# A decoder layer whose first projection (v) gets leading transposes, a paired tile order, VectorE sums and a separate pool for two convolution tiles

## The chip, the cores and the metric

The kernel runs on one core of a Trainium2 chip. The metric is device time in microseconds (us) of one execution; lower is better. TensorE multiplies matrices into the eight banks of PSUM, VectorE and ScalarE do element-wise work, GpSimd does element-wise work on SBUF only, and SyncE (SP) issues every DMA of this kernel, in order, in one queue. Within each engine instructions run in a fixed order.

## The reference, cut to what matters

One layer: a combined input projection of x (1024 tokens x 1024), differential attention with four heads beside a short gated convolution, an output projection, a layer norm, a gated feed-forward part and a second layer norm, all in float32. The change touches the first step, the columns of v:

```python
proj = jnp.einsum('bsd,dc->bsc', x, w_in)                # 1024 x 3072
q, k = proj[..., :512], proj[..., 512:1024]
v = proj[..., 1024:1536].reshape(bsz, s, 4, 128)         # the step that is changed
o = diff_attention(q, k, v, lam)
conv_out = gate_b * causal_dwconv(gate_c * hc, conv_w)   # u = gate_c*hc, w = the convolution
x = layer_norm(alpha * x + concat([o, conv_out]) @ w_out)
x = layer_norm(alpha * x + ffn(x))
```

## The kernel before, in words

**Number format.** Each float32 operand is split into a high part in TensorE's reduced format and a low part that is the rest: ScalarE copies the high part (L61), VectorE subtracts (L62). `mm3` (L67) then issues three matmuls, high x high (L70), high x low (L71), low x high (L72). Each streams 512 columns.

**Strassen-like products.** All projections but v's are done in 2x2 blocks with seven products (`pair`, L95). They need x^T in seven forms, `xb` (names `11`, `t1`, `t2`, `22`, `t3`, `21`, `t4`), each with high and low part: blocks of x^T and sums of such blocks. Tokens 0 to 511 (tiles t = 0 to 3) and tokens 512 to 1023 (tiles t = 4 to 7) are the two halves in one direction, k blocks 0 to 3 and 4 to 7 the two halves in the other.

**The stage of v** (L173 to L273) goes first, because it makes `xb` on its way. w_v is loaded in four pieces of two k blocks (`load_wv`, L181, three raw buffers, so the fourth piece waits until the first one is split), x^T in eight token tiles of 512 KB. `x_operands(t)` (L199) splits both halves of token tile t: for t < 4 straight into `xb` 11 and 21, for t of 4 and up into a tile `b12` (two buffers) and into `xb` 22. `v_mm` issues the three matmuls of tile t and block k, so a tile takes 8 x 3 = 24 matmuls and the stage 192. `v_out` (L237) evacuates a finished tile in two parts (ScalarE, then VectorE) and sends both to DRAM. `x_combine(t)` (L214), for t of 4 and up, subtracts tiles t and t-4 from each other four times (GpSimd, `tmp`, L221) and splits each result into `xb` t1 to t4 (ScalarE, VectorE): four subtractions and four splits for each of four tiles.

Tiles 0 and 1 run interleaved over k while w_v comes in (L261 to L264); then tiles 2 to 7 follow one by one, with `x_combine(4)` to `x_combine(7)` behind the tile that they belong to. The order of instructions on each engine is made when the program is built, by a list scheduler: of what is ready by its own estimate of time, an engine takes what stands first in the program.

**What follows.** `project` (L312) for head 0: its first operand `a` (a tile of the ring in pool `wab`, L78) is split out of a raw weight tile and multiplies `xb` 11 into X, twelve matmuls; the second product, into Z, multiplies `xb` t1 by the sum `s` (L113). Pools of the stage of v (`ini`) are given back at L296, and the pools `qk`, `at`, `wab`, `kz` (L299 to L302) are stacked over the same addresses, so their first writers wait for the last readers of the `ini` tiles that lay there. An x tile takes 4 KB in each partition, and so do `u` and `w` of the convolution (L441, L456), which lie in `at`, ahead of `wab`. In this layout the ring's first tile lies over x tiles 7 and 6, and `klo1` (L325) over x tiles 7 and 0.

Of the kernel before, what the change touches and what calls it, by code (L numbers as in the profile page):

```python
# [8 lines left out]
F32 = mybir.dt.float32  # L9
# [3 lines left out]
ALU = mybir.AluOpType  # L13
# [3 lines left out]
P = 128  # L17
S = 1024
D = 1024
NT = S // P  # L20
NK = D // P
# [8 lines left out]
NEG = -1e30  # L30
NKEEP = 3
NEARLY = 4
FIN = 5
OWED = (0, 1)
NTHIRD = 7
# [9 lines left out]
def layer_kernel(ctx: ExitStack, tc: tile.TileContext, x, xt, w_in, w_v, lam, vecs, w_out, ln, w_up, w_down, out):  # L45
    nc = tc.nc
    V, A, T, G = nc.vector, nc.scalar, nc.tensor, nc.gpsimd
    SQ = nc.sync

    def pool(name, stack=None, side=None, space=None, **kw):  # L50
        args = dict(name=name, bufs=1, reuse_waits="tile")
        if space is not None:
            args["space"] = space
        if side is not None:
            args["side"] = side
        return (stack or ctx).enter_context(tc.tile_pool(**args))

    def split(hi, lo, src, scale=None, eng=None):

        if scale is None:  # L60
            A.copy(hi, src)  # L61
            (eng or V).tensor_tensor(lo, src, hi.bitcast(F32), op=ALU.subtract)  # L62
        else:
            A.mul(hi, src, scale)
            V.scalar_tensor_tensor(lo, src, scale, hi.bitcast(F32), op0=ALU.mult, op1=ALU.subtract)
# [81 lines left out]
    ident = const.tile([P, P], F32, name="ident")  # L147
# [15 lines left out]
    xop_st, ab = ExitStack(), ExitStack()  # L163
# [3 lines left out]
    p_tr = pool("p_tr", ab, space=PSUM)  # L167
# [5 lines left out]
    st0 = ExitStack()  # L173
    ini = pool("ini", st0, side="right")
    p_in = pool("p_in", st0, space=PSUM, side="right")
    xs = [ini.tile([P, NK, P], F32, name=f"xt{t}", tag="xt", bufs=NT) for t in range(NT)]
    wv = []

    NRAW = 3
# [1 line left out]
    def load_wv(k0):  # L181
        raw = wraw.tile([P, 2, 512], F32, name=f"wv{k0}_r", tag="wr", bufs=NRAW)
        w_ = ini.tile([P, 2, 2, 512], F32R, name=f"wv{k0}_s", tag="wv", bufs=4)
        wv.extend((w_[:, 0, i, :], w_[:, 1, i, :]) for i in range(2))
        parts = ((0, 1), (1, 2)) if k0 == 0 else ((0, 2),)

        def load(i):
            a, b = parts[i]
            SQ.dma_start(raw[:, a:b, :], w_v[:, k0 + a:k0 + b, :])
            split(w_[:, 0, a:b, :], w_[:, 1, a:b, :], raw[:, a:b, :])  # L190

        return load
# [4 lines left out]
    vparts = {}  # L197

    def x_operands(t, halves=(0, 1)):  # L199
        vp = vparts.get(t) or [None] * NK  # L200
        for i in halves:
            src = xs[t][:, 4 * i:4 * i + 4, :]
            ts = slice(t % 4 * P, (t % 4 + 1) * P)
            n = ("11", "21") if t < 4 else (None, "22")
            if n[i]:
                put(n[i], ts, src)
                vp[4 * i:4 * i + 4] = [[xb[n[i]][c][:, k, ts] for c in range(2)] for k in range(4)]
            else:
                b12 = ini.tile([P, 2, 4, P], F32R, name=f"b12_{t}", tag="b12", bufs=2)
                split(b12[:, 0], b12[:, 1], src)  # L210
                vp[4 * i:4 * i + 4] = [[b12[:, c, k, :] for c in range(2)] for k in range(4)]
        vparts[t] = vp

    def x_combine(t):  # L214
        ts = slice((t - 4) * P, (t - 3) * P)
        lo_, hi_ = xs[t][:, 0:4, :], xs[t][:, 4:8, :]
        b11, b21 = xs[t - 4][:, 0:4, :], xs[t - 4][:, 4:8, :]

        def tmp(n, a, b):
            v = ini.tile([P, 4, P], F32, name=n, tag=n if n in ("t1", "t2") else "t34", bufs=2)  # L220
            G.tensor_tensor(v, a, b, op=ALU.subtract)  # L221
            return v

        t1 = tmp("t1", lo_, b11)
        put("t1", ts, t1)
        t2 = tmp("t2", hi_, t1)
        put("t2", ts, t2)
        t3 = tmp("t3", hi_, lo_)
        put("t3", ts, t3)
        t4 = tmp("t4", b21, t2)  # L230
        put("t4", ts, t4)
# [8 lines left out]
        for c in range(2):  # L240
            SQ.dma_start(v_d[c][:, :, t, :], vs[:, c, :].bitcast(F32).rearrange("p (h d) -> p h d", h=H))

    pv_ = [p_in.tile([P, 512], F32, name=f"vps{t}", tag="v", bufs=4) for t in range(NT)]
    for t in range(NT):
        vparts[t] = None
    load0 = load_wv(0)
    load0(0)
    SQ.dma_start(xs[0][:, 0:4, :], xt[0][:, 0:4, :])
    x_operands(0, (0,))
    load0(1)  # L250
    SQ.dma_start(xs[0][:, 4:8, :], xt[0][:, 4:8, :])
    SQ.dma_start(xs[1], xt[1])
    x_operands(1, (0,))
    x_operands(0, (1,))
    load_wv(2)(0)
    x_operands(1, (1,))
    load_wv(4)(0)
    load_wv(6)(0)
    for t in range(2, NT):
        SQ.dma_start(xs[t], xt[t])  # L260
    for k0 in (0, 1, 2, 4, 6):  # L261
        for t in (0, 1):
            for k in ((k0,) if k0 < 2 else (k0, k0 + 1)):
                v_mm(pv_[t], t, k)  # L264
    for t in (0, 1):
        v_out(pv_[t], t)
    for t in range(2, NT):
        x_operands(t)
        for k in range(NK):
            v_mm(pv_[t], t, k)  # L270
        v_out(pv_[t], t)
        if t >= 4:
            x_combine(t)  # L273


    cols = const.tile([P, vecs.shape[1]], F32, name="cols")
# [22 lines left out]
    qk = pool("qk", ab, side="right")  # L299
    at = pool("at", ab, side="right")  # L300
    wp = pool("wab", ab, side="right")
    kz = pool("kz", ab, side="right")  # L302

    def wpair(f0, f1, src, pl, tags, bufs):
# [133 lines left out]
                post.append(lambda c=c, qi=qi, pm=pm, pa=pa: spread(c, qi, pm, pa))  # L438

    def convolve(j):  # L440
        w = at.tile([P, S], F32, name=f"w{j}", tag="w")  # L441
        u = us[j]
        V.tensor_scalar(w, u[:, 2:S + 2], cw(2, j), None, op0=ALU.mult)
        V.scalar_tensor_tensor(w, u[:, 1:S + 1], cw(1, j), w, op0=ALU.mult, op1=ALU.add)
        V.scalar_tensor_tensor(w, u[:, 0:S], cw(0, j), w, op0=ALU.mult, op1=ALU.add)
        ws[j] = w
# [6 lines left out]
    us, ws = {}, {}  # L453

    def new_u(j):
        us[j] = at.tile([P, S + 2], F32, name=f"u{j}", tag="u")  # L456
        G.memset(us[j][:, 0:2], 0.0)
        return us[j][:, 2:514], us[j][:, 514:S + 2]

# [119 lines left out]
    for t0 in (0, 3, 6):  # L579
        tt = list(range(t0, min(t0 + 3, NT)))  # L580
        w = len(tt) * P
# [60 lines left out]
    for a in rows_:  # L642
        norm(*a)
    for f in range(NEARLY):
        if f >= NEARLY - 2:
            turn(*rows_[f - NEARLY + 2])
        wg, X, Y = wgate(f), bank(f"X{f}"), bank(f"Y{f}")
# [3 lines left out]
        block_product(e0, Y, None, hb, "21", True, parts(e0, wg[:, 4:8, :], G))  # L651
        c11 = gp.tile([P, 512], F32, name=f"c11_{f}", tag="c11", bufs=NEARLY)
        V.tensor_tensor(c11, Y, p1, op=ALU.add)
# [27 lines left out]
    for f in range(NF):  # L681
# [14 lines left out]
        if f == NF - 1:  # L696
            w2 = e1.tile([P, 2, 512], F32, name="b11_0", tag="wu", bufs=2)
            for i in range(2):
                w = w2[:, i, :]
# [138 lines left out]
    for j in range(HK + 2):  # L838
        if j < HK:
            op = ready.pop(0) if ready else (operand(a11[j], "S", j), operand(b11[j], "T", j))  # L840
            for t in range(4):
                mm_row(X, op, t, j == 0, j == HK - 1)
        if j >= 2:
            i = j - 2
            op = (operand(add(a21[i], a22[i], ALU.add), "S", i),
                  operand(add(b12[i], b11[i], ALU.subtract), "T", i))
# [34 lines left out]
    def done_p7(t):  # L881
# [3 lines left out]
    product(X, lambda i: a21[i], lambda i: b12[i], False, done=done_p7, prompt=True,  # L885
            after={FIN + t: (lambda t=t: finish(t, r11[t], r12[t])) for t in range(4)})

# [50 lines left out]
```

## Time and profile before

| | us |
|---|---|
| median of 3 runs (1133.85 to 1134.67) | 1134.52 |
| the profiled execution: its own time | 1134.1 |
| the profiled execution: its span, first to last instruction | 1132.3 |
| TensorE busy in the span | 1084.2 |
| stage of v: first to last matmul | 5.12 to 62.44 |

The span is what the trace covers; the profiled run's own time is 1.8 us longer. Everything below is read from that one execution, in us from the start of its span. A matmul's shown duration includes its way through the pipeline; the rate is read from the spacing of starts.

### The profile page before, as it was taken

The page shows a single profiled execution, that of the slowest core. Times are in us where ns is not written, and L with a number is a line of the kernel's source. Part 1 is how long each engine was busy: PE and PEld are TensorE (multiplying, and loading weights), DVE is VectorE, ACT ScalarE, POOL GpSimd, SP SyncE. Part 2 cuts the span into 40 slices and gives each one's busy share as a digit, 9 for nine tenths or more (in the row PEclk, how much of TensorE's full clock was granted, in tenths as well). Part 3 has the DMA queues.
Part 4 walks back from the last instruction along what each step waited for, and adds up shares of the span by engine and source line. Part 5 has one row for each costly group of instructions (what it writes and reads, how often), then busy time and mean ns, then how long its engine had stood idle before and what let it go on. Part 6 is the DMA issues. An engine that isn't in the chain of part 4 may idle for free.

```text
span 1132.3 us, 13828 instructions
## 1 busy us (share of the span) xinstructions
PE 1084.2 (96%) x4924; PEld 870.9 (77%) x4924; DVE 913.2 (81%) x1377; ACT 522.1 (46%) x980; POOL 174.4 (15%) x198
## 2 busy tenths in 40 slices
PE   7899999999999999789999999999999999999997
PEld 5676777877768888567888888888888887788885
DVE  7868889779887688998977777777777589997797
ACT  6347677377576333444433333333333333444550
POOL 4601313013132214860000000000000000000102
PEclk9899999999999999999999999999999999999999
DMA  7431111211204765422331313121222196121111
GB/s 264 133 112 38 45 68 47 83 57 47 80 28 160 259 200 190 153 75 93 111 112 57 112 56 111 58 104 64 97 71 93 59 381 237 38 65 38 38 75 75
DMA packets 50278, 118.53 MB, mean 105 GB/s; under 512 B 5025, under 2 KB 18465, under 8 KB 50209
## 3 DMA queue, kind: packets, MB, share of 16 engines
q1 hardware_dynamic: 50208, 117.64, 30.1%
q8 instruction: 39, 0.64, 0.2%
q14 instruction: 31, 0.25, 0.1%
HBM read 90.88 MB, written 26.74 MB: 104 GB/s over the span
## 4 chain that ended last, share of the span: by engine, by line
PE 66%; DVE 18%; ACT 6%; DMA 4%; POOL 4%; issue 2%; SPq 0%; POOLq 0%; DVEq 0%; ACTq 0%
PE X L70 8%; PE X L72 8%; PE X L71 8%; PE Z L72 5%; PE Z L71 5%; PE Z L70 5%; PE dx L71 2%; PE dx L72 2%; PE dx L70 2%; PE op L70 2%; PE op L72 2%; PE op L71 2%; DVE a L62 2%; PE dz L70 2%; PE dz L71 2%
## 5 line engine op out<-in xcount | busy, mean ns | idle before, releaser
L62 DVE TENSOR_TENSOR a<-s,a 128x512 fp32r<-128x512 f32 x118 | 85.3, 724 | 45.2 <-ACT a L61 44.2
L61 ACT CAST a<-s 128x512 fp32r<-128x512 f32 x118 | 73.4, 623 | 94.5 <-PE X L72 40.0
L61 ACT CAST a<-w 128x512 fp32r<-128x512 f32 x106 | 65.9, 623 | 87.1 <-PE X L72 40.8
L62 DVE TENSOR_TENSOR a<-w,a 128x512 fp32r<-128x512 f32 x102 | 72.3, 709 | 20.4 <-ACT a L61 20.0
L61 ACT CAST T<-b 128x512 fp32r<-128x512 f32 x66 | 40.6, 622 | 68.4 <-PE dz L72 34.0
L71 PE MATMUL dx<-T,S 128*128 128x512 f32 x176 | 69.1, 392 | 1.2 <-DVE T L62 1.2
L72 PE MATMUL dx<-T,S 128*128 128x512 f32 x176 | 68.5, 389 | 0.0
L70 PE MATMUL dx<-T,S 128*128 128x512 f32 x176 | 66.0, 390 | 0.0
L688 POOL MEMSET gs<- 128x2 f32 x22 | 2.2, 99 | 379.4 <-DVE t L707 379.4
L62 DVE TENSOR_TENSOR T<-b,T 128x512 fp32r<-128x512 f32 x66 | 45.2, 687 | 16.6 <-ACT T L61 16.6
L72 PE MATMUL op<-wo,cl 128*128 128x512 f32 x128 | 51.0, 398 | 5.7 <-DVE cl L62 5.7
L423 DVE TENSOR_REDUCE nm<-sc 128x1 f32<-128x128 f32 (+5 forms) x64 | 47.4, 749 | 7.7 <-PE sc L422 7.1
L71 PE MATMUL dz<-T,S 128*128 128x512 f32 x132 | 51.8, 393 | 0.0
L72 PE MATMUL dz<-T,S 128*128 128x512 f32 x132 | 51.4, 390 | 0.0
L70 PE MATMUL op<-wo,ch 128*128 128x512 f32 x128 | 51.1, 399 | 0.0
L427 ACT ACTIVATE p<-sc,nm 128x128 f32<-128x128 f32 (+5 forms) x64 | 47.6, 745 | 7.2 <-DVE p L436 4.0
L71 PE MATMUL op<-wo,ch 128*128 128x512 f32 x128 | 50.5, 395 | 0.0
L70 PE MATMUL dz<-T,S 128*128 128x512 f32 x132 | 48.4, 394 | 0.5 <-ACT T L61 0.4
L708 ACT ACTIVATE t<-t 128x1024 f32<-128x1024 f32 x22 | 23.4, 1062 | 51.2 <-DVE t L707 51.2
L345 POOL TENSOR_TENSOR me<-me,y 128x256 f32<-128x256 f32 x16 | 12.5, 784 | 216.8 <-ACT y L344 216.8
L420 PE MATMUL sc<-k,q 128*128 128x512 f32 (+2 forms) x96 | 37.1, 394 | 7.6 <-ACT p L427 6.1
L61 ACT CAST wo<-wo_r 128x512 fp32r<-128x512 f32 x40 | 24.4, 619 | 40.4 <-PE op L72 37.8
(312 smaller groups left out, 3403.3 us busy)
## 6 DMA issues: line engine op xcount, KB each, us to landing
w<-in_w_up SPq DMA_DIRECT2D x44, 512.0 KB, 3.4
b<-in_w_down SPq DMA_DIRECT2D x44, 256.0 KB, 6.8
w<-in_w_in SPq DMA_DIRECT2D x20, 512.0 KB, 3.4
wo_r<-in_w_out SPq DMA_DIRECT2D x20, 512.0 KB, 4.7
act_d<-act SPq DMA_DIRECT2D x19, 512.0 KB, 2.6
ra<-act_d SPq DMA_DIRECT2D x19, 512.0 KB, 7.5
v_d<-vs SPq DMA_DIRECT2D x16, 256.0 KB, 2.6
vhl<-v_d SPq DMA_DIRECT2D x8, 512.0 KB, 4.7
```

The costliest lines, as they stand in the source:

```text
L61: A.copy(hi, src)
L62: (eng or V).tensor_tensor(lo, src, hi.bitcast(F32), op=ALU.subtract)
L70: T.matmul(ps, lh, rh, start=first, stop=False, **kw)
L71: T.matmul(ps, lh, rl, start=False, stop=False, **kw)
L72: T.matmul(ps, ll, rh, start=False, stop=last, **kw)
L345: G.tensor_tensor(me, me, y, op=ALU.mult)
L420: T.matmul(sc[:, bs], q2[m][:, qs], k2[m][:, bs], start=True, stop=False)
L423: V.tensor_reduce(nm[:, m:m + 1], sc[:, :n], axis=AX.X, op=ALU.max, negate=True)
L427: A.activation(pt[:, :n], sc[:, :n], AF.Exp, bias=nm[:, m:m + 1], accum_out=sm[:, m:m + 1])
L688: G.memset(gs[:, 0:2], 0.0)
L708: A.activation(t_, t_, AF.Silu)
```

## The change

- `xs` is allocated in the order `VORDER` = 0, 4, 1, 5, 2, 6, 3, 7; PSUM banks of v's tiles are allocated where a tile begins (`bank_of`) instead of all at once.
- Sixteen transposes of the identity matrix (128 x 128, float32) into a PSUM tile that nobody reads stand ahead of the first load.
- The interleaved pair is tiles 0 and 4, where it was 0 and 1. Their first halves are loaded ahead of w_v's second piece, their second halves behind it. The remaining tiles follow in `VORDER`.
- The operands of the next tile are split ahead of the matmuls of a tile; `x_combine(4)`, `(5)`, `(6)` and `(7)` come ahead of the matmuls of tiles 1, 2, 3 and 7.
- The subtractions in `x_combine` run on VectorE, where they ran on GpSimd.
- `u` and `w` are allocated in a new pool `uw` between `wab` and `kz`.

```diff
@@ -30,6 +30,8 @@
 NEG = -1e30
 NKEEP = 3
 NEARLY = 4
+VORDER = (0, 4, 1, 5, 2, 6, 3, 7)
+NWARM = 16
 FIN = 5
 OWED = (0, 1)
 NTHIRD = 7
@@ -173,7 +175,7 @@
     st0 = ExitStack()
     ini = pool("ini", st0, side="right")
     p_in = pool("p_in", st0, space=PSUM, side="right")
-    xs = [ini.tile([P, NK, P], F32, name=f"xt{t}", tag="xt", bufs=NT) for t in range(NT)]
+    xs = {t: ini.tile([P, NK, P], F32, name=f"xt{t}", tag="xt", bufs=NT) for t in VORDER}
     wv = []
 
     NRAW = 3
@@ -218,7 +220,7 @@
 
         def tmp(n, a, b):
             v = ini.tile([P, 4, P], F32, name=n, tag=n if n in ("t1", "t2") else "t34", bufs=2)
-            G.tensor_tensor(v, a, b, op=ALU.subtract)
+            V.tensor_tensor(v, a, b, op=ALU.subtract)
             return v
 
         t1 = tmp("t1", lo_, b11)
@@ -240,37 +242,55 @@
         for c in range(2):
             SQ.dma_start(v_d[c][:, :, t, :], vs[:, c, :].bitcast(F32).rearrange("p (h d) -> p h d", h=H))
 
-    pv_ = [p_in.tile([P, 512], F32, name=f"vps{t}", tag="v", bufs=4) for t in range(NT)]
-    for t in range(NT):
-        vparts[t] = None
+    pv_ = {}
+
+    def bank_of(t):
+        pv_[t] = p_in.tile([P, 512], F32, name=f"vps{t}", tag="v", bufs=4)
+
+    def load_x(t, halves=(0, 1)):
+        for i in halves:
+            SQ.dma_start(xs[t][:, 4 * i:4 * i + 4, :], xt[t][:, 4 * i:4 * i + 4, :])
+
+
+    wt = p_tr.tile([P, 4, P], F32, name="wt", tag="tr", bufs=1)
+    for i in range(NWARM):
+        T.transpose(wt[:, i % 4, :], ident, ident)
+    for t in (0, 4):
+        bank_of(t)
     load0 = load_wv(0)
     load0(0)
-    SQ.dma_start(xs[0][:, 0:4, :], xt[0][:, 0:4, :])
+    load_x(0, (0,))
     x_operands(0, (0,))
     load0(1)
-    SQ.dma_start(xs[0][:, 4:8, :], xt[0][:, 4:8, :])
-    SQ.dma_start(xs[1], xt[1])
-    x_operands(1, (0,))
+    load_x(4, (0,))
+    x_operands(4, (0,))
+    load_wv(2)(0)
+    load_x(0, (1,))
+    load_x(4, (1,))
     x_operands(0, (1,))
-    load_wv(2)(0)
-    x_operands(1, (1,))
+    x_operands(4, (1,))
     load_wv(4)(0)
     load_wv(6)(0)
-    for t in range(2, NT):
+    for t in VORDER[2:]:
         SQ.dma_start(xs[t], xt[t])
     for k0 in (0, 1, 2, 4, 6):
-        for t in (0, 1):
+        for t in (0, 4):
             for k in ((k0,) if k0 < 2 else (k0, k0 + 1)):
                 v_mm(pv_[t], t, k)
-    for t in (0, 1):
+    for t in (0, 4):
         v_out(pv_[t], t)
-    for t in range(2, NT):
-        x_operands(t)
+    x_operands(VORDER[2])
+    for n, t in enumerate(VORDER[2:], 2):
+        bank_of(t)
+        if n + 1 < NT:
+            x_operands(VORDER[n + 1])
+        if n % 2 == 0:
+            x_combine(VORDER[n - 1])
+        elif n == NT - 1:
+            x_combine(t)
         for k in range(NK):
             v_mm(pv_[t], t, k)
         v_out(pv_[t], t)
-        if t >= 4:
-            x_combine(t)
 
 
     cols = const.tile([P, vecs.shape[1]], F32, name="cols")
@@ -299,6 +319,7 @@
     qk = pool("qk", ab, side="right")
     at = pool("at", ab, side="right")
     wp = pool("wab", ab, side="right")
+    uw = pool("uw", ab, side="right")
     kz = pool("kz", ab, side="right")
 
     def wpair(f0, f1, src, pl, tags, bufs):
@@ -438,7 +459,7 @@
                 post.append(lambda c=c, qi=qi, pm=pm, pa=pa: spread(c, qi, pm, pa))
 
     def convolve(j):
-        w = at.tile([P, S], F32, name=f"w{j}", tag="w")
+        w = uw.tile([P, S], F32, name=f"w{j}", tag="w")
         u = us[j]
         V.tensor_scalar(w, u[:, 2:S + 2], cw(2, j), None, op0=ALU.mult)
         V.scalar_tensor_tensor(w, u[:, 1:S + 1], cw(1, j), w, op0=ALU.mult, op1=ALU.add)
@@ -453,7 +474,7 @@
     us, ws = {}, {}
 
     def new_u(j):
-        us[j] = at.tile([P, S + 2], F32, name=f"u{j}", tag="u")
+        us[j] = uw.tile([P, S + 2], F32, name=f"u{j}", tag="u")
         G.memset(us[j][:, 0:2], 0.0)
         return us[j][:, 2:514], us[j][:, 514:S + 2]
 
```

## Rows read from the trace of the kernel before

**Rows 1.** The page, part 1: busy time and share of the span, instructions.
```profile
PE 1084.2 (96%) x4924; PEld 870.9 (77%) x4924; DVE 913.2 (81%) x1377; ACT 522.1 (46%) x980; POOL 174.4 (15%) x198
```

**Rows 2.** Stretches of the stage of v: bounds, length, busy time of each engine, granted clock.
```profile
5.10:12.90 7.80, 6.60 (x13) 4.01 (x14) 4.77 (x8) 4.47 (x6) 0.00 (x0) 1.00 0.99 361
...
21.10:43.60 22.50, 22.48 (x97) 17.84 (x96) 22.36 (x20) 10.62 (x19) 20.35 (x13) 1.00 0.50 149
43.60:54.10 10.50, 5.55 (x12) 3.94 (x13) 8.93 (x16) 3.97 (x8) 4.46 (x4) 0.67 0.36 98
```

**Rows 3.** Timeline of TensorE, stage of v: start, duration, line, operation, idle before.
```profile
20.91 0.40 PE L72 MATMUL vps<-wv_s,xb_21l 128*128 128x512 f32 x1
...
43.19 0.40 PE L72 MATMUL vps<-wv_s,xb_22l 128*128 128x512 f32 x1
47.39 0.80 PE L70 MATMUL vps<-wv_s,b 128*128 128x512 f32 x1 [3.81 <-ACT b L61]
...
54.12 0.39 PE L70 MATMUL vps<-wv_s,xb_22h 128*128 128x512 f32 x1
```

**Rows 4.** Timeline of ScalarE around the gap of TensorE.
```profile
46.20 0.62 ACT L61 CAST xb_t4h<-t 128x512 fp32r<-128x512 f32 x1 [0.57 <-POOL t L221]
46.72 0.61 ACT L61 CAST b<-xt 128x512 fp32r<-128x512 f32 x1
```

**Rows 5.** GpSimd and VectorE, groups by shape from 0 to 62.5 us: busy, mean ns.
```profile
L221 POOL TENSOR_TENSOR t<-xt,t 128x512 f32<-128x512 f32 x8 | 13.5, 1683 | 0.3
...
L62 DVE TENSOR_TENSOR xb_22l<-xt,xb_22h 128x512 fp32r<-128x512 f32 x4 | 7.1, 1770 | 0.0
```

**Rows 6.** Timeline of VectorE while GpSimd stands still.
```profile
41.49 0.68 DVE L62 TENSOR_TENSOR xb_t2l<-t,xb_t2h 128x512 fp32r<-128x512 f32 x1
42.09 0.68 DVE L62 TENSOR_TENSOR xb_t3l<-t,xb_t3h 128x512 fp32r<-128x512 f32 x1
```

**Rows 7.** Timeline of TensorE, first matmuls.
```profile
5.12 0.80 PE L70 MATMUL vps<-wv_s,xb_11h 128*128 128x512 f32 x1 [5.12 <-ACT xb_11h L61]
...
9.76 0.79 PE L70 MATMUL vps<-wv_s,xb_11h 128*128 128x512 f32 x1 [1.18 <-ACT xb_11h L61]
...
11.63 0.63 PE L71 MATMUL vps<-wv_s,xb_11h 128*128 128x512 f32 x1
...
12.06 0.63 PE L72 MATMUL vps<-wv_s,xb_11l 128*128 128x512 f32 x1
...
13.21 0.40 PE L71 MATMUL vps<-wv_s,xb_11h 128*128 128x512 f32 x1
```

**Rows 8.** Timeline of ScalarE and VectorE at the loads.
```profile
7.83 0.62 ACT L61 CAST xb_21h<-xt 128x512 fp32r<-128x512 f32 x1 [1.25 <-DMA xt<-in_xt]
...
11.45 3.83 DVE L62 TENSOR_TENSOR wv_s<-wv_r,wv_s 128x1024 fp32r<-128x1024 f32 x3 [0.41 <-ACT wv_s L61]
```

**Rows 9.** Timelines: the identity on GpSimd; later transposes on TensorE.
```profile
1.17 0.29 POOL masks.py:199 TENSOR_SCALAR_AFFINE_SELECT ident<-ident 128x128 f32<-128x128 f32 x1
...
421.21 1.04 PE L531 MATMUL trp<-ident,xr 128*128 128x128 f32 x8
```

**Rows 10.** A later stretch at the low clock: columns as in the stretches above.
```profile
502.00:504.00 2.00, 2.00 (x6) 1.56 (x5) 1.66 (x2) 1.42 (x3) 2.00 (x2) 0.50 0.00 0
```

**Rows 11.** Timelines of TensorE and ScalarE from the last tile of v on.
```profile
62.21 0.40 PE L72 MATMUL vps<-wv_s,xb_22l 128*128 128x512 f32 x1
63.80 0.50 PE L70 MATMUL X<-xb_11h,a 128*128 128x512 f32 x1 [1.19 <-ACT a L61]
...
67.64 0.40 PE L70 MATMUL Z<-xb_t1h,a 128*128 128x512 f32 x1
...
63.12 0.62 ACT L61 CAST a<-w 128x512 fp32r<-128x512 f32 x1
```

**Rows 12.** Timelines of VectorE and GpSimd: the last reader of x tile 7.
```profile
51.97 0.68 DVE L62 TENSOR_TENSOR b<-xt,b 128x512 fp32r<-128x512 f32 x1
...
52.71 0.94 POOL L325 MEMSET klo<- 64x1024 f32 x1 [5.54 <-DVE b L62]
```

## The prediction

> **What bounds the kernel now.** The page's busy shares come first: TensorE is busy 96% of the span [rows 1]. So a gain can only come from the few stretches where it isn't, or where it runs slowly. The stretches of the stage of v show two of them [rows 2]. From 5.1 to 12.9 us TensorE is busy 6.60 of 7.80 us but gets through only some 13 matmuls; from 43.6 to 54.1 us it is busy 5.55 of 10.50 us, at a granted clock of 0.67. Between the two, from 21.10 to 43.60, it is busy 22.48 of 22.50 us: there it is the bound.
>
> The timeline of TensorE prices the second one [rows 3]. From 20.91 (the 48th matmul, last of tile 1) to 43.19 (the 144th, last of tile 5) 96 matmuls take 22.28 us, so a start comes every 0.232 us. The next one, first of tile 6, should start at 43.42 and starts at 47.39; the thirteenth after 43.19 should start at 43.19 + 13 x 0.232 = 46.21 and starts at 54.12. That is 7.9 us lost. The first part of it is a wait for ScalarE, which splits x tile 6 (`b`) at 46.72, directly behind `xb_t4h` at 46.20, which waited for GpSimd [rows 4]. The tile's buffer had long been free; it stood behind `x_combine` in ScalarE's queue, and `x_combine` was late because its sixteen subtractions take 1.68 us each on GpSimd and VectorE's splits take 1.77 us beside them [rows 5]. While GpSimd stands still the same split takes 0.68 us and the next starts 0.60 us later [rows 6]. The second part is the clock: after the pause TensorE runs at its lower level.
>
> A third loss lies behind the last tile: the last matmul of v starts at 62.21 and ends its slot at 62.44, but the second product of `project` (Z) starts at 67.64 where twelve matmuls of X need 2.8 us [rows 11]. So 5.2 - 2.8 = 2.4 us go there, because ScalarE splits the first `a` at 63.12, after the last evacuation.
>
> I take the start of Z, 67.64 us, as the mark: what is gained up to there is kept if the work behind it is unchanged, and it is: same instructions, TensorE bound.
>
> **The start, with tiles 0 and 4.** The first matmul starts at 5.12, when the first pieces are there [rows 7]; the order of the first three transfers is unchanged, so this stays. The fourth transfer, half an x tile, is used at 7.83 [rows 8]; it was tile 0's second half and now is tile 4's first, so the second tile can go on about 8.5 us (split 0.62 us) instead of 9.76 [rows 7]. w_v's second piece now comes behind 1.5 MB, not 2.0 MB; at the 361 GB/s of this stretch [rows 2] that is 1.45 us earlier. The low parts of the last three pieces ran back to back from 11.45 on, 3.83 / 3 = 1.28 us each [rows 8]; the first of them ended at 12.73 and now ends between 11.3 and 12.7. The last ended at 15.28 and stays there, since the bytes ahead of it are the same 3 MB. From the second piece on 35 matmuls of the pair are left (one of its 36 needs no low part): at 0.232 us they take 8.1 us, and they end at 19.4 (bound 20.9), later than the loads ask for. Before, the pair ended at 21.14. I take 19.4, as the engines that split have idle time there: ScalarE is busy 4.47 of 7.80 us.
>
> **The transposes.** Eight later transposes take 1.04 us with the tail of the last [rows 9]. This trace has no transposes by themselves, so the price is bounded. Eight in 1.04 us are at most 0.13 us each at the high clock, twice that at the low one: 16 x 0.26 = 4.2 us. They can begin when the identity is written, at 1.46 [rows 9], and end at 5.6, half a microsecond behind the place of the first matmul; this is absorbed, since the first twelve matmuls have until 11.3 us. If each took as long as the first matmul, 0.80 us [rows 7], they would end at 14.3, and 48 matmuls at 0.232 us at 25.4: 6.0 us late, 1129.3. I take nothing, the nearer row being that of transposes. What they are to give is the clock. Before, starts stand 0.43 us apart at 11.63 and 12.06, which is 512 columns at 1.2 GHz, and from 13.21 on they run at 2.4 GHz [rows 7]: 33 starts from there to 20.91 [rows 3], 0.233 us apart. (The granted clock reads 1.00 in this first stretch, but the spacing is that of the later stretch that reads 0.50 [rows 2, 10].) It rose after TensorE had been at work without a pause from 9.76. In the new order it works with hardly a pause from 5.12, and the transposes lengthen this at its front. So I take the high clock by 11.3.
>
> **The tiles behind the pair.** 144 matmuls x 0.232 = 33.4 us, if nothing stops them: 19.4 + 33.4 = 52.8. What could stop them is VectorE, which gets the sixteen subtractions. Per pair of tiles it has 4 splits of x, 4 subtractions, 4 splits of sums and 2 evacuations, 14 operations of one shape; at 0.60 us that is 8.4 us beside 24 x 2 x 0.232 = 11.1 us of TensorE. As a whole, 12 splits of x, 32 operations of `x_combine` and 8 evacuations, 52 x 0.60 = 31.2 us from 15.3, end at 46.5. So the subtractions are free, hidden by TensorE's 33.4 us, and the splits come back from 1.77 to 0.68 us because GpSimd stands still. A subtraction ahead of a split in VectorE's queue holds the split, and TensorE behind it: one or two subtractions among the low parts of the loads cost up to 1.2 us, evacuations that wait for TensorE ahead of a split up to 1; I take 0.8 together. The two buffers of `b12` are free when tile 6 and tile 7 want them: tile 4 is done in the pair, tile 5 as the second after it. The stall of 7.9 us has then no cause: `x_operands` of tile 6 stands well ahead in ScalarE's queue and hangs on no slow chain.
>
> SP's queue gets the same transfers. Those of `v_out` follow the evacuations as before, and the reload of v is asked for well ahead of its first use in either order.
>
> **The pool.** Before, the ring's first tile lay over x tiles 7 and 6. Tile 7's last reader on VectorE is at 51.97, and GpSimd's `klo`, which lies over it as well, waits for that one [rows 12]. Without `u` and `w` ahead of it, `wab` moves up by 8 KB, two x tiles: the ring's first tile then lies over x tiles 2 and 6, whose last readers are in `x_combine(6)`, some 12 us ahead of the end of the stage. `s` comes to lie partly over w_v's first piece, read last by the sixth matmul of tile 7, 4.2 us before the end, and needs some 2 us to become an operand: in time. So X can begin without a pause: 52.8 + 2.8 = 55.6 is the start of Z, plus 0.8 is 56.4.
>
> **The sum.** 67.64 - 56.4 = 11.2 us: 1.7 at the start, 7.9 from the stall (with its clock), 2.4 behind the last tile, less 0.8. Against the profiled execution's 1134.1 this is 1122.9; the median is 0.4 above it, so 1123.3.
>
> **Rivals.**
> The transposes don't raise the clock, and it rises at 12.9 as before. Between 11.3 and 12.9 then 3.7 matmuls run, and the other 31.3 end at 20.2: 0.8 us, or 2.2 us if the rise came at 16.0. About 1124.3. For it: no stretch of this trace shows what transposes alone do to the clock. Against it: the second tile's matmuls come earlier anyway. The Trainium skill, TensorE: Matmul & The Clock Gate, Part 4: PE-mode transpose, says that the high clock doesn't engage for transposes, since they don't count as work in the same way. By that rule the time is this rival's; the trace neither agrees nor differs.
>
> The first `a` still stands behind the last evacuation in ScalarE's order, so that the pool brings nothing: 2.4 us back, 1125.7.
>
> A wait of the same kind takes the place of the one removed: the built order puts a split behind an evacuation or a sum that the chip finishes late, TensorE pauses once for about 4 us and its clock falls. Price as in [rows 3], 7.9 us: 1131.2. Against it: the order before was undone by durations of 1.7 us that GpSimd brought about, and these go.
>
> VectorE becomes the bound. With a spacing p the 52 operations end at 15.3 + 52p. They hold up Z from p = 0.78 us on, and make the kernel slower than before from p = (67.64 - 15.3) / 52 = 1.01 us on; at 1.2 us Z starts at 77.7, 10.1 us later than before: 1144.6. For it: VectorE's mean is 1.77 us in [rows 5]. Against it: 0.60 us whenever GpSimd stands still [rows 6], and after the change it does.
>
> The gain is given back: a later transfer or a new order behind the stage of v holds Z's successors where they were. About 1134.5. I know of no row that speaks for it.
>
> **How the numbers follow.** Forecast 0.50, clock 0.15, first `a` 0.12, new pause 0.10, given back 0.07, VectorE 0.06. The likeliest time is 1123.3. Without the slack of 0.8 us, and with a slot or two more behind the stage, it could be 1120; the new pause ends at 1131.2, so 1120 to 1131.5 holds the first four cases but for their edges, a little over 8 in 10. A measurement here tells about 0.2%, 2.3 us, from no change: all of the first four are faster by more than that (0.87), given back is the same (0.07), VectorE slower (0.06).
>
> **What would show it.** In the new profile: starts 0.23 us apart at 11.3 us or not (clock); the pair's last matmul at 19 to 20 us; no pause of TensorE and no fall of the clock up to X; VectorE's splits at 0.68 us throughout; GpSimd idle from 2 us on; Z starting at about 56 us. I am wrong if VectorE's operations stay above 0.8 us, if one is queued behind a late evacuation, or if the stretches behind Z are not shifted by one and the same amount.

## The result, and the profile after

| | before | after |
|---|---|---|
| median, us (5 runs each, taken together) | 1134.67 (1133.85 to 1136.88) | 1129.07 (1126.70 to 1129.10) |
| ratio, 95% interval | 1 | 0.9936 [0.9923, 0.9949] |
| the profiled execution: its own time | 1134.1 | 1129.07 |
| its span | 1132.3 | 1127.3 |
| 49th matmul of v starts | 21.15 | 22.09 |
| last matmul of v starts | 62.21 | 55.23 |
| X starts | 63.80 | 56.87 |
| Z starts | 67.64 | 61.95 |

The change makes the kernel 5.6 us faster. The likeliest time of the prediction, 1123.3, was 5.8 us too low: half of the expected gain did not come. The marks tell where. Z comes 5.69 us earlier, which is -0.94 at the start (49th matmul), +7.92 between the 49th and the last matmul of v, and -1.29 from there to Z. What is gained at Z is kept but for 0.7 us: the span is 5.0 us shorter.

The page after, part 1, answers [rows 1]: TensorE has the same work and sixteen transposes more, and GpSimd's time has gone from 174.4 to 147.6 us.

```profile
PE 1084.9 (96%) x4940; PEld 873.8 (78%) x4940; DVE 906.4 (80%) x1393; ACT 522.5 (46%) x980; POOL 147.6 (13%) x182
```

The stretches of the kernel after, columns as in [rows 2], with two more at the end:

```profile
5.10:12.90 7.80, 6.21 (x25) 4.76 (x26) 5.88 (x10) 4.98 (x8) 0.00 (x0) 1.00 0.94 342
21.10:43.60 22.50, 22.50 (x98) 18.24 (x98) 21.65 (x37) 13.49 (x24) 1.71 (x3) 1.00 0.66 196
43.60:54.10 10.50, 10.50 (x47) 8.49 (x46) 3.20 (x10) 1.38 (x3) 0.00 (x0) 1.00 0.35 100
54.10:62.50 8.40, 6.49 (x21) 4.51 (x20) 5.17 (x8) 2.55 (x5) 0.00 (x0) 0.80 0.47 136
59.40:62.40 3.00, 3.00 (x9) 2.32 (x8) 2.10 (x4) 0.73 (x2) 0.00 (x0) 0.50 0.65 194
```

The stall is gone: from 43.60 to 54.10 TensorE is busy all of 10.50 us at a clock of 1.00, where it was 5.55 at 0.67. Where v ends there is a new loss: from 59.40 to 62.40 the granted clock is 0.50.

VectorE by groups from 0 to 62.5 us (busy, mean ns of one | idle before), against [rows 5]:

```profile
L223 DVE TENSOR_TENSOR t<-xt,t 128x512 f32<-128x512 f32 x8 | 5.5, 683 | 0.0
L64 DVE TENSOR_TENSOR xb_22l<-xt,xb_22h 128x512 fp32r<-128x512 f32 x4 | 2.7, 684 | 0.0
```

A subtraction takes 0.68 us on VectorE (1.68 on GpSimd before), and a split beside it 0.68 us (1.77 before).

The 49th matmul of v, in the kernel before and in the kernel after:

```profile
21.15 0.40 PE L70 MATMUL vps<-wv_s,xb_11h 128*128 128x512 f32 x1
```

```profile
22.09 0.40 PE L72 MATMUL vps<-wv_s,xb_11h 128*128 128x512 f32 x1
```

TensorE's timeline at the start, against [rows 7]:

```profile
5.31 0.80 PE L72 MATMUL vps<-wv_s,xb_11h 128*128 128x512 f32 x1 [5.31 <-ACT xb_11h L63]
...
8.34 0.79 PE L72 MATMUL vps<-wv_s,b 128*128 128x512 f32 x1 [1.38 <-ACT b L63]
...
10.21 0.63 PE L73 MATMUL vps<-wv_s,xb_11h 128*128 128x512 f32 x1
10.64 2.30 PE L257 MATMUL wt<-ident 128*128 128x128 f32 x16
12.69 0.48 PE L74 MATMUL vps<-wv_s,xb_11l 128*128 128x512 f32 x1
13.01 0.40 PE L72 MATMUL vps<-wv_s,b 128*128 128x512 f32 x1
```

The sixteen transposes stand first in the program but ninth in TensorE's order, behind eight matmuls of v. There they hold v's next matmul back by 12.69 - 10.64 = 2.05 us; and the first matmuls run as slowly as before (0.80, 0.79, 0.63 us).

TensorE and then ScalarE from the last tile of v on, against [rows 11]:

```profile
55.23 0.40 PE L74 MATMUL vps<-wv_s,xb_22l 128*128 128x512 f32 x1
56.87 0.50 PE L72 MATMUL X<-xb_11h,a 128*128 128x512 f32 x1 [1.24 <-ACT a L63]
...
58.27 0.51 PE L74 MATMUL X<-xb_11h,a 128*128 128x512 f32 x1 [0.68 <-DVE a L64]
...
59.08 0.51 PE L74 MATMUL X<-xb_11h,a 128*128 128x512 f32 x1
59.39 0.63 PE L72 MATMUL X<-xb_11h,a 128*128 128x512 f32 x1
59.82 0.63 PE L73 MATMUL X<-xb_11l,a 128*128 128x512 f32 x1
...
61.95 0.63 PE L72 MATMUL Z<-xb_t1h,a 128*128 128x512 f32 x1
```

```profile
55.71 0.58 ACT L63 CAST vs<-vps 128x512 fp32r<-128x512 f32 x1 [4.94 <-PE vps L74]
56.19 0.62 ACT L63 CAST a<-w 128x512 fp32r<-128x512 f32 x1
```

ScalarE is idle for 4.94 us, evacuates the last tile (`vs`), and only then splits the first `a`. So TensorE waits as it did before, once for the high part (1.64 us from start to start, 1.59 before) and once for the low part; and then X's starts stand 0.43 us apart, which is 512 columns at 1.2 GHz. Before, X ran at 2.4 GHz in spite of the same two waits.

### The profile page after: what moved, and what is told of

The parts are those of the page before. It is cut to its first block, busy times and chain, and to the rows that moved or that the text cites. A ratio compares the mean times of both kernels' runs of the same rounds, so it can differ in the third digit from the quotient of the medians.

```text
span 1127.3 us, 13854 instructions
## 1 busy us (share of the span) xinstructions
PE 1084.9 (96%) x4940; PEld 873.8 (78%) x4940; DVE 906.4 (80%) x1393; ACT 522.5 (46%) x980; POOL 147.6 (13%) x182
## 4 chain that ended last, share of the span: by engine, by line
PE 71%; DVE 15%; ACT 5%; POOL 3%; DMA 3%; issue 2%; SPq 0%; POOLq 0%; DVEq 0%; ACTq 0%
PE X L74 8%; PE X L72 8%; PE X L73 8%; PE Z L74 5%; PE Z L73 5%; PE Z L72 5%; PE dx L73 2%; PE dx L74 2%; PE dx L72 2%; PE op L74 2%; PE op L73 2%; PE op L72 2%; DVE a L64 2%; PE dz L74 2%; PE dz L72 2%
```

## The experiments

Theory after the result: the gain is the end of GpSimd's subtractions and nothing else. The transposes cost time because they stand amid v's matmuls; the pool brings nothing because the order of ScalarE, not an address, holds the first `a`; and the clock falls in the pause ahead of X. Rivals: the new order of tiles has a share in the 7.9 us; the transposes don't lift the clock wherever they stand; the pool does help and something else hides it; the loss ahead of Z is not the pause. Unless it is said, a kernel computes all that the reference has. The experiments' own marks, each from its profiled execution:

| kernel | median, us | ratio to before, 95% interval | 49th of v | last of v | X | Z | span |
|---|---|---|---|---|---|---|---|
| changed kernel again | 1127.53 | 0.9935 [0.9916, 0.9954] | 21.91 | 55.05 | 56.69 | 60.54 | 1123.8 |
| no transposes | 1127.50 | 0.9938 [0.9921, 0.9954] | 20.41 | 53.55 | 55.19 | 60.58 | 1125.4 |
| transposes really first | 1126.20 | 0.9926 [0.9909, 0.9943] | 20.65 | 53.82 | 55.41 | 59.25 | 1123.8 |
| first operand ahead | 1132.04 | 0.9973 [0.9961, 0.9984] | 22.74 | 55.89 | 56.12 | 60.27 | 1130.3 |
| before, sums on VectorE | 1128.22 | 0.9943 [0.9927, 0.9958] | 21.03 | 54.13 | 55.76 | 61.15 | 1126.0 |
| changed, sums on GpSimd | 1129.99 | 0.9954 [0.9940, 0.9968] | 25.05 | 58.20 | 59.79 | 63.63 | 1128.5 |
| changed, no pool `uw` | 1127.09 | 0.9931 [0.9914, 0.9948] | 22.50 | 55.65 | 57.29 | 61.13 | 1126.6 |
| no transposes, filled pause | 1125.16 | 0.9914 [0.9898, 0.9930] | 20.98 | 54.13 | 55.76 | 59.61 | 1123.4 |
| before, sums on VectorE, filled | 1125.99 | 0.9920 [0.9895, 0.9946] | 20.76 | 53.84 | 55.48 | 59.31 | 1124.2 |
| transposes first, and filled | 1126.41 | 0.9925 [0.9903, 0.9946] | 20.69 | 53.85 | 55.45 | 59.30 | 1124.7 |

From Z to the end of the span all but one take 1063.3 to 1065.5 us (1064.7 before, 1065.4 after), so Z is a fair mark to within 2 us; the exception, the kernel with the first operand ahead, is told below.

**The changed kernel again.** No edit.

> The changed kernel once more, on the chip of the next three runs, as their yardstick. In its profile the sixteen transposes ran at 10.64 to 12.69 us, in the middle of the matmuls, and the clock was at 2.4 GHz behind them. If what differs between its five executions (1126.7 to 1129.1 us) is the clock around the pause behind v (the spacing of X's matmuls was 0.43 us from 59.39 to 62.38 in the profiled one), executions with X at 0.23 us spacing throughout are about 2 us shorter. If the difference lies elsewhere, X looks the same and the time differs all the same.

Its four runs are 1125.60, 1125.97, 1129.10 and 1129.49: one program, two levels 3.5 us apart. The profiled run is on the lower one (1125.60), the one of the section above on the upper (1129.07), so the two traces price the gap. First its stretch from v's end to Z; then the stretch from 480 to 520 us of the kernel after, and of this run:

```profile
54.10:62.50 8.40, 6.49 (x27) 4.63 (x26) 5.17 (x8) 2.73 (x5) 0.00 (x0) 1.00 0.48 140
```

```profile
480.00:520.00 40.00, 33.97 (x141) 27.02 (x140) 35.80 (x47) 16.94 (x30) 16.15 (x12) 0.91 0.22 79
```

```profile
480.00:520.00 40.00, 35.27 (x157) 27.59 (x156) 37.54 (x50) 19.06 (x32) 16.20 (x13) 1.00 0.24 81
```

With the same pauses ahead of X as the run above (56.69 - 55.05 = 1.64 us), the clock holds at 1.00 here, where it was 0.80. Z comes 1.41 us earlier, 0.18 of that from the last matmul of v and the other 1.23 from this clock; behind Z another 2.1 us go between 365 and 905 us, where of all stretches of 20 us only those from 480 to 520 differ in clock (0.91 and 1.00). Together that is the 3.5 us. So the fall of the clock ahead of Z is not a feature of the program but of the execution, and so is part of the miss.

**No transposes, and transposes really first.**

```diff
-NWARM = 16
+NWARM = 0
```

> The changed kernel without the sixteen transposes, nothing else changed. Theory 1, they are a plain cost where they stand: the matmul that stood behind them starts at 10.64 instead of 12.69, the 49th matmul comes 1 to 2 us earlier than 22.09, and the kernel gets 1 to 2 us faster than the changed one. Rival, they are what lifted the clock: the spacing of starts stays 0.43 us beyond 13 us; if it lasts until 16 us, some 12 matmuls take 0.2 us more each, and the 49th is no earlier than 22.0: same time or slower.

```diff
-        T.transpose(wt[:, i % 4, :], ident, ident)
+        last = T.transpose(wt[:, i % 4, :], ident, ident).ins
...
-                v_mm(pv_[t], t, k)
+                with tc.issue_after(last):
+                    v_mm(pv_[t], t, k)
```

> The changed kernel with TensorE's order of v's first tiles fixed behind the transposes, so that these really stand ahead of the first matmul. Theory, transposes lift the clock like other work: they run from 1.5 to about 5 us, the first matmuls start at 5.1 to 5.6 and stand 0.23 us apart from about 8 us on, the 49th starts before 20.5. [...]

TensorE's first matmuls without transposes, and then with the transposes ahead of all of them:

```profile
5.37 0.79 PE L72 MATMUL vps<-wv_s,xb_11h 128*128 128x512 f32 x1 [5.37 <-ACT xb_11h L63]
...
12.21 0.46 PE L72 MATMUL vps<-wv_s,b 128*128 128x512 f32 x1
12.50 0.39 PE L73 MATMUL vps<-wv_s,xb_11h 128*128 128x512 f32 x1
```

```profile
1.52 3.37 PE L257 MATMUL wt<-ident 128*128 128x128 f32 x16 [1.52 <-POOL ident masks.py:199]
5.33 0.50 PE L72 MATMUL vps<-wv_s,xb_11h 128*128 128x512 f32 x1 [0.44 <-ACT xb_11h L63]
5.67 0.39 PE L73 MATMUL vps<-wv_s,xb_11h 128*128 128x512 f32 x1
...
7.88 0.79 PE L72 MATMUL vps<-wv_s,b 128*128 128x512 f32 x1 [1.33 <-ACT b L63]
8.47 0.63 PE L73 MATMUL vps<-wv_s,b 128*128 128x512 f32 x1
...
11.20 0.43 PE L73 MATMUL vps<-wv_s,b 128*128 128x512 f32 x1
```

Transposes do lift the clock: behind them the first matmul takes 0.50 us and the second 0.39, where they take 0.80 and 0.63 in the other order. The row of the transposes merges sixteen instructions; in the trace their starts stand 0.21 us apart up to 4.35 us and 0.11 us from 4.50 on, so the clock rose while TensorE did nothing but transposes. But TensorE then waits 1.33 us for tile 4's half, and from 7.88 on it is back at the lower level until 11.2:

```profile
7.90:11.00 3.10, 3.10 (x7) 2.20 (x8) 2.27 (x4) 2.33 (x4) 0.00 (x0) 0.50 1.06 381
```

The granted clock of this stretch is 0.50, and the forecast of 0.23 us between starts from about 8 us on did not come. So nothing is left of it for the sum: the 49th matmul starts at 20.65, against 20.41 without any transposes (20.98 in the run with the filled pause below, which begins in the same way). Where the change puts them, at 22.09 or 21.91, they cost 0.9 to 1.7 us. In the times that is not to be told apart: the three kernels' intervals overlap, and the run without transposes lost its lead at once, as the clock fell in X (Z at 60.58, against 60.54 in the repeat).

**The first operand ahead.** The first `a` gets a slot in the pool of raw weights, which is open from the start, and is split before v ends.

```diff
+        if ahead:
+            v11 = wraw.tile([P, 2, 4, P], F32R, name="a0", tag="wr", bufs=NRAW)
+            split(v11[:, 0], v11[:, 1], wa[:, 0:4, :])
...
-        qa, qb, ka, kb = project(h, H + h)
+        qa, qb, ka, kb = project(h, H + h, ahead=h == 0)
```

> The changed kernel with the first operand of the first projection behind v (the split of the first half of its weights) in a tile of the pool of raw weights, which is open from the start, instead of the ring that is opened when the stage of v is given back. Theory: not the address but the closing of v's pools sets that split behind v's last evacuation; with it out of the way X starts 0.23 us behind the last matmul of v, and only the pause ahead of Z is left, about 1.2 us (evacuation of X 0.6 and split of s 0.6 stand ahead of it): Z starts at about 59.5 instead of 61.95, and the kernel is 2 to 3 us faster than the changed one. Rival: something else holds X, a load or the PSUM bank: no change.

TensorE at the end of v, and the longest wait behind it:

```profile
55.89 0.40 PE L74 MATMUL vps<-wv_s,xb_22l 128*128 128x512 f32 x1
56.12 0.40 PE L72 MATMUL X<-xb_11h,a 128*128 128x512 f32 x1
...
60.27 0.50 PE L72 MATMUL Z<-xb_t1h,a 128*128 128x512 f32 x1 [1.19 <-ACT a L63]
...
105.59 0.58 PE L362 MATMUL mq<-sqh,ones 128*128 128x256 f32 x1 [3.73 <-ACT sqh L63]
```

Here it does what the theory says: X starts 0.23 us behind the last matmul of v, and Z follows that matmul by 4.38 us, where it was 6.72 in the kernel after and 5.49 in its repeat. One pause has gone and the other has moved ahead of Z. But the kernel as a whole is 3 to 4.5 us slower than the changed one: from Z to the end of the span it takes 1070.0 us, not 1063.3 to 1065.5. The instructions behind Z stand in another order, and at 105.59 TensorE has waited 3.73 us for a square on ScalarE. ScalarE's timeline tells what held the square, first in this run, then the same copy in the kernel after:

```profile
103.55 0.37 ACT L423 COPY osb<-o 128x256 f32<-128x256 f32 x1 [3.58 <-DMA cat_d<-osb]
...
105.12 0.42 ACT L63 CAST sqh<-sq 128x256 fp32r<-128x256 f32 x1
```

```profile
106.65 0.37 ACT L419 COPY osb<-o 128x256 f32<-128x256 f32 x1 [1.57 <-DMA cat_d<-osb]
```

`osb` is a finished block of the attention, and the square is made from it. It has one buffer, so its copy waits until the block before has gone to DRAM. In this run ScalarE stands still for 3.58 us before the copy, and the square and TensorE's matmul come late by that; in the kernel after the copy stands behind more of ScalarE's work, the wait is 1.57 us, and TensorE doesn't wait for the square. A local gain was given back by the new order 45 us later. That this one copy is the whole of the 5 us is not shown, nor whether the slot that `a0` takes from the raw weights has a share.

**One part at a time: the sums.**

```diff
-            G.tensor_tensor(v, a, b, op=ALU.subtract)
+            V.tensor_tensor(v, a, b, op=ALU.subtract)
```

in the kernel before (first), and the reverse in the changed kernel (second).

> The kernel before with one edit: the sixteen subtractions of x on VectorE. Theory, the pause before tile 6 came from GpSimd's durations alone: VectorE's splits take 0.68 us throughout, TensorE goes from the 49th matmul (21.1 us) to the last of v without a pause at 0.232 us, so the last one starts at about 54.3 instead of 62.21, Z at about 59.7 instead of 67.64, and the kernel is 7.9 us faster than before, which is more than the whole change brought in its profiled execution (5.0 us). Rival, the paired order is needed too, because the split of tile 6 waits for a buffer of b12 that tile 4 gives back only at 35 us and it may still be queued behind the sums: a pause of 2 to 8 us stays.

> The changed kernel with the sixteen subtractions back on GpSimd. Theory as in the run before: GpSimd takes 1.7 us each, VectorE's splits beside them 1.77 us, 36 or so of them between 15 and 50 us, and a split that TensorE waits for comes late: pauses of 3 to 8 us in v, last matmul of v at 58 to 63, kernel slower than the changed one by that. Rival, the order alone (operands split one tile ahead, halves paired) hides it: last matmul of v at about 55, time as the changed kernel.

The kernel before with that one line, TensorE at the end of v; then VectorE's group of subtractions:

```profile
54.13 0.40 PE L72 MATMUL vps<-wv_s,xb_22l 128*128 128x512 f32 x1
55.76 0.50 PE L70 MATMUL X<-xb_11h,a 128*128 128x512 f32 x1 [1.24 <-ACT a L61]
```

```profile
L221 DVE TENSOR_TENSOR t<-xt,t 128x512 f32<-128x512 f32 x8 | 5.5, 684 | 0.0
```

From the 49th matmul (21.03) to the last (54.13) it takes 33.10 us, 143 spacings of 0.231 us: no pause. The one line brings the ratio to 0.9943 [0.9927, 0.9958], against 0.9936 [0.9923, 0.9949] for the whole change. All else in the diff adds nothing that these intervals can tell. Z comes at 61.15, not at the 59.7 forecast: the clock fell in X here too.

The reverse, the changed kernel with GpSimd's sums: TensorE in the load, and the groups of VectorE (from 5 to 25 us) and GpSimd (from 5 to 62 us):

```profile
19.58 0.50 PE L73 MATMUL vps<-wv_s,xb_21h 128*128 128x512 f32 x1 [2.00 <-DVE wv_s L64]
```

```profile
L64 DVE TENSOR_TENSOR wv_s<-wv_r,wv_s 128x1024 fp32r<-128x1024 f32 x3 | 4.7, 1580 | 0.2 <-ACT wv_s L63 0.2
...
L223 POOL TENSOR_TENSOR t<-xt,t 128x512 f32<-128x512 f32 x8 | 13.9, 1739 | 4.6 <-DVE xb_t4l L64 3.1 <-DVE xb_t2l L64 1.3
```

From the 49th matmul (25.05) to the last (58.20) it also takes 33.15 us. So the new order by itself removes the stall too, with the subtractions still on GpSimd: behind the 49th matmul none of the theory's pauses came. But it lets them begin in the load, where VectorE's splits of w_v then take 1.58 us instead of 1.22 and TensorE waits 2.00 us for one. The start is 3 us later, and by that alone the last matmul lies in the theory's range of 58 to 63. The two edits remove the same 7.9 us, each for itself; together they bring it once. The order alone is worth less in the end (0.9954 [0.9940, 0.9968]), by that start.

**The pool.**

```diff
-    uw = pool("uw", ab, side="right")
...
-        w = uw.tile([P, S], F32, name=f"w{j}", tag="w")
+        w = at.tile([P, S], F32, name=f"w{j}", tag="w")
...
-        us[j] = uw.tile([P, S + 2], F32, name=f"u{j}", tag="u")
+        us[j] = at.tile([P, S + 2], F32, name=f"u{j}", tag="u")
```

> The changed kernel with u and w back in the pool they had. Theory: the pool brings nothing, since the first split behind v is ordered behind the closing of v's pools and not by an address: X starts 1.6 us behind v's last matmul as it does with the pool, and the time is that of the changed kernel within 1 us but for the clock around that pause. Rival, as the prediction had it, the address matters: X starts later, by up to the 3 us that tile 7's last reader stands behind x_combine(6).

ScalarE's split of the first `a`, and TensorE's wait for it:

```profile
56.61 0.62 ACT L63 CAST a<-w 128x512 fp32r<-128x512 f32 x1
```

```profile
57.29 0.50 PE L72 MATMUL X<-xb_11h,a 128*128 128x512 f32 x1 [1.24 <-ACT a L63]
```

X starts 1.64 us behind the last matmul of v (55.65), to the hundredth as with the pool, and the time is that of the repeat within 0.5 us. The address is not what holds the split: here VectorE's last subtraction of x tiles starts at 42.51, 14 us ahead of it.

**The pause filled.** No leading transposes; twelve between the last matmul of v and X, which compute nothing that is used.

```diff
-NWARM = 16
+NWARM = 0
...
-            v_mm(pv_[t], t, k)
+            end = v_mm(pv_[t], t, k)
+        if n == NT - 1:
+            with tc.issue_after(end):
+                for i in range(12):
+                    T.transpose(wt[:, i % 4, :], ident, ident)
```

> The changed kernel without the sixteen leading transposes, and with twelve transposes between the last matmul of v and X, where TensorE waits for the first operand anyway (1.6 us). Theory: executions of one program differ by 2 to 3.5 us because the clock falls in that pause in some and not in others; with TensorE at work in it X and the first product into Z stand 0.23 us apart in every execution, so Z starts 2 us earlier than in the run without transposes (60.58), at about 58.5, and the spread of the executions shrinks below 2 us. Rival: transposes don't keep the clock up, or the spread has another place (about 500 us, where TensorE waits as well): X at 0.43 us, or a spread as before.

```profile
54.36 1.47 PE L296 MATMUL wt<-ident 128*128 128x128 f32 x12
55.76 0.50 PE L72 MATMUL X<-xb_11h,a 128*128 128x512 f32 x1
...
57.17 0.50 PE L74 MATMUL X<-xb_11h,a 128*128 128x512 f32 x1 [0.67 <-DVE a L64]
...
59.61 0.39 PE L72 MATMUL Z<-xb_t1h,a 128*128 128x512 f32 x1
```

The transposes fill the whole pause, X comes no earlier than without them (1.63 us behind), and the clock holds: Z at 59.61, a microsecond later than forecast, since v ended later and the second pause stayed. Its four runs lie between 1124.52 and 1126.01, within 1.5 us, where the repeat's lie within 3.9. The closer times speak for the filler, but the trace by itself doesn't: with the pause unfilled the clock held up to Z in five of the eight profiled executions (before, the repeat, transposes first, sums on GpSimd, no pool) and fell in three.

**What the pairing is worth, and both repairs.** The same twelve transposes in the kernel before with sums on VectorE; and in the changed kernel with its sixteen really first. The edit of the former:

```diff
-            G.tensor_tensor(v, a, b, op=ALU.subtract)
+            V.tensor_tensor(v, a, b, op=ALU.subtract)
...
-            v_mm(pv_[t], t, k)
+            end = v_mm(pv_[t], t, k)
+        if t == NT - 1:
+            wt = p_tr.tile([P, 4, P], F32, name="wt", tag="tr", bufs=1)
+            with tc.issue_after(end):
+                for i in range(12):
+                    T.transpose(wt[:, i % 4, :], ident, ident)
```

> The kernel before, with two edits: x's sums on VectorE only, and twelve identity transposes on TensorE between v's last tile and X (they compute nothing that is used). It keeps the old order of v's tiles, so against the run with the pairs and the same twelve transposes (1125.2 us) it tells what the pairing is worth. Theory (pairing is worth nothing once VectorE keeps up): 49th matmul of v near 21.0, last tile from about 54.1, X at 0.23 us spacing, Z near 59.6, and 1125 to 1126 us. Rival (the old order still leaves TensorE waiting for splits halfway): last tile 1 us or more later with a pause of TensorE between its 49th and 193rd matmul, and 1126.5 us or more.

> The changed kernel with both repairs: the sixteen transposes really ahead of v's first matmul, and twelve more between v's last tile and X. Theory (start and end are separate terms that add): 49th matmul near 20.6 as in the run with the transposes first, X at 0.23 us spacing right behind the fill, Z near 59.0, and 1124.5 to 1125.5 us. Rival (the start is set by the arrival of the raw tiles and the splits, not by the clock): 49th near 21.0, Z near 59.6 and the 1125.2 us of the run with the fill alone.

With the old order of tiles the 49th matmul starts at 20.76 and Z at 59.31; with the pairs at 20.98 and 59.61. The pairing is worth nothing that these runs can tell once VectorE keeps up. With both repairs the 49th starts at 20.69, as forecast, but Z at 59.30, and the median of 1126.41 is no better. One line of that run tells why the early clock is of so little use:

```profile
8.62 0.80 PE L72 MATMUL vps<-wv_s,b 128*128 128x512 f32 x1 [2.10 <-ACT b L63]
```

TensorE waits 2.10 us for tile 4's half, and the clock has fallen again. So the load has a share in the start, as the rival had it, and the lower clock behind it has another; neither forecast came as a whole. All three filled kernels end X at the full clock. The clearest pair is the kernel before with sums on VectorE, without and with the filler alone: Z at 61.15 and 59.31, 1128.22 and 1125.99 us, but the intervals of the ratios overlap. The filled kernels' medians (1125.16, 1125.99, 1126.41) are three of the four lowest here, but their intervals overlap with the changed kernel's too: that they are faster than it is likely and not shown.

## Why the prediction was right, and where it was wrong

**The tiles behind the pair: right.** 144 matmuls were to take 33.4 us; they take 55.23 + 0.23 - 22.09 = 33.37. The term of 7.9 us came out as 7.92. The cause was right as well: splits at 0.68 us as soon as GpSimd stands still [rows 5, 6]. The 0.8 us of slack for VectorE's queue were not needed. What the prediction left out is that the new order removes the stall without the moved line, too: either would have done.

**The start: the term was mis-sized, +1.7 forecast and -0.94 measured.** The step that failed is the one on the transposes. It took their place in the program for their place on TensorE ("they can begin when the identity is written") and so counted them as hidden. The front of the document says how the order is made, by a list scheduler, and the prediction didn't ask what that would do with sixteen instructions that nobody waits for. They came ninth and took 2.05 us of the stream. The rest of the miss is the clock: "the high clock by 11.3" came at 12.2 without the transposes, and the 49th matmul at 20.41, not 19.4; in the run with the filled pause, with the same beginning, at 13.4 and 20.98. Had they stood first it would have come to about the same, as the transposes' own runs show (20.65, 20.69). A slip without effect: "behind 1.5 MB, not 2.0 MB" counts w_v's second piece itself; 1.0 and 1.5 MB stand ahead of it, and the difference of 1.45 us is right.

The Trainium skill, TensorE: Matmul & The Clock Gate, Part 4: PE-mode transpose, says that the high clock doesn't engage for transposes. The run with the transposes first disagrees: their starts go from 0.21 to 0.11 us apart while nothing else runs, and behind them the first matmuls take 0.50 and 0.39 us, not 0.80 and 0.63. The trace shows these transposes as MATMUL with float32 operands; whether another form behaves otherwise, no run here shows. The rival built on that rule (1124.3) named a wrong cause, though its result, no gain from the transposes, came true.

**Behind the last tile: wrong, +2.4 forecast and -1.29 measured.** The prediction followed the address ("the pool"), and no run shows a wait for it. Its own rows spoke against one: x tile 7's last reader on VectorE starts at 51.97 and takes 0.68 us [rows 12], and the first `a` is split at 63.12 [rows 11], ten us later. ScalarE works in a fixed order, and the first `a` stands behind the last evacuation in either kernel, as the row of ScalarE above shows with 4.94 us of idle time ahead of that evacuation. This was the second rival ("the first `a` still stands behind the last evacuation"), which had 0.12 and should have been the forecast: nothing in the diff moves that split. The two pauses cost what they cost before: 1.64 - 0.23 = 1.41 us ahead of X and 5.08 - 12 x 0.232 = 2.30 from X to Z, where the clock has a share: the seven spacings from 59.08 to 61.95 take 2.87 us, not 1.62, so 1.25 us is the clock and 1.05 the second pause and its restart. Before, the pauses were 1.36 and 1.06 [rows 11], and no clock fell.

**The sum.** Of the 5.55 us by which Z was forecast too early (56.4 for 61.95), 2.64 are the start, 3.69 the end, less the 0.8 of slack. That the mark carries to the time was right to 0.7 us. That 1129.07 lies inside the range is in part luck: two terms missed to the same side, and the upper end, 1131.5, had been drawn for a new pause in v that did not come.

**The other rivals.** No new pause took the place of the stall (10.50 of 10.50 us busy from 43.60 on); VectorE did not become the bound (its timeline has the last sum's split at 43.90, in front of eleven more us of v on TensorE); behind Z no more than 0.7 us was given back in the changed kernel, but it was in the one with its first operand ahead, by the very mechanism that was named, a new order.

**Open:** what decides in one execution that the clock holds through the pause ahead of X and in another that it falls; and what the 5 us behind Z in the kernel with the first operand ahead hold beyond the 3.73 us of that one wait.

## What to carry to other kernels

An instruction's place in the program is not its place on the engine where a scheduler makes the order: ask of every added instruction what it depends on and what would hold it at the place meant. Before an address is blamed for a wait, look at what stands ahead of the waiting instruction on its own engine; a buffer that comes free earlier moves nothing there. And when a change has several parts that aim at the same wait, one line may bring it all: here the subtractions on VectorE alone.

## What the runs showed of the hardware

Sixteen float32 transposes of 128 x 128 (1.52 to 4.89 us) bring TensorE to its higher clock: matmuls right behind them take 0.50 and 0.39 us instead of 0.80 and 0.63, and after a wait of 1.33 us for a load behind three such matmuls it is at the lower one (granted clock 0.50 from 7.9 to 11.0). Twelve of them (1.47 us) in the pause behind v left the clock high in all three kernels that had them, which three traces alone don't prove to be their work. With the pause unfilled it stayed high in five of eight profiled executions and fell in three (1.00 and 0.80 in the same stretch of two executions of one program), and this and one further stretch around 500 us account for the 3.5 us between the two levels of its times. A subtraction or a split of 128x512 float32 takes VectorE 0.68 us while GpSimd stands still; beside GpSimd's subtractions, of 1.68 us each, a split takes 1.77.
